# RG-LRU gates as four 64x64 quadrants of the TensorE array in place of 128x128 block-diagonal products

## The chip, the cores and the metric

One NeuronCore of a Trainium2 chip runs the whole program as one launch. The metric is the device time of an execution in microseconds (us); a comparison uses the median of several executions. Engines are named as in the profile: PE is TensorE (PEld its weight loads), DVE is VectorE, ACT is ScalarE, SP is SyncE, which issues the transfers here.

## What is computed

The reference is one inference step of a two-layer decoder trunk, with 1,024 prompt tokens and 8 sample tokens (1,032 columns in all), width 1,024, all in float32. Layer 0 has an SSD mixer and a gMLP mixer, layer 1 a Conformer convolution and an RG-LRU. The change concerns the two gates of the RG-LRU:

```python
xc, buf_new = _causal_dwconv(xd, conv_buf, conv_w, conv_b)
xb = xf.reshape(bsz, L, D_HEADS, D_BLOCK)          # 16 heads of 64 channels
r = sigmoid(einsum('blhi,hij->blhj', xb, wa).reshape(bsz, L, W) + ba)
i = sigmoid(einsum('blhi,hij->blhj', xb, wx).reshape(bsz, L, W) + bx)
log_a = -LRU_C * r * softplus(-lam)
a = exp(log_a)
bterm = sqrt(-expm1(2.0 * log_a)) * (i * xf)
# h[t] = a[t] * h[t-1] + bterm[t], then the gate path and the output projection
```

Each head has its own 64x64 weight matrix for `r` and for `i`.

## The kernel before

Activations lie channel by channel: a tile has 128 channels on its partitions and the 1,032 tokens along it. The tokens are cut into three chunks of 344 columns (`CH`). The large projections are done by `unit` and `chunk` (lines 107 to 123): for each block of 128 output channels, and each chunk, 24 products of 128x128 by 344 columns run into one PSUM bank (`mm_...`, lines 115 to 117). They are three products for each of eight blocks of input channels, since inputs and weights are split into a rounded part and the rest. Four banks belong to these (`mm`), two each to the pools `sA` and `sB`.

Layer 1 alternates over eight blocks of 128 channels (`ORDER`, line 27): `c_block(j)` for the Conformer convolution (projections `gb` and `ga`, then a convolution of 31 taps, L859, that VectorE does at low priority) and `d_block(j)` for the RG-LRU (projections `xd` and `gd`, a convolution of 4 taps, the gates, the scan). A block of 128 channels holds two heads. So lines 809 to 818 build `bd`, a 128x128 block-diagonal matrix for each gate and block, out of a memset and 32 transfers of 64x64, and `d_block` does for each gate `m` and chunk `c` one product of 128x128 and one activation (lines 880 to 885), through a bank of `sA`:

```python
pg = bank("sA", f"gt{j}{m}{c}")
T.matmul(pg[:, :CH], bd[:, m, j % 4, :], xc[:, cs], start=True, stop=True)
S.activation(t[:, cs], pg[:, :CH], AF.Sigmoid, bias=pcol(bn, j))
```

The tile framework orders each engine's instructions by priority and by its own estimate of when they are ready; the order is fixed when the program is built. The products of the gates of block `j` thus stand among those of `c_block(j + 1)`.

Two other places have products that use a part of the array. `ssd_group` in layer 0 (lines 459 to 464) writes head `h` to partitions 0 to 63 or 64 to 127 of the tile `py`, by `h % 2`: a product of 128 rows and 64 columns with `x0` (L462) and, from the second chunk on, one with the state `st` (L464). And `csT` (line 412) has 16 columns:

```python
dst = py[r0:r0 + 64, (h // 2) * P:(h // 2 + 1) * P]
T.matmul(dst, x0[:, h, :], cb_b[:, h, :], start=True, stop=c == 0)
if c:
    T.matmul(dst, st[:, h * 64:(h + 1) * 64], ce[:, h, :], start=False, stop=True)
```

After the eight blocks come the sums over the convolution's channels (`sum_cln`, lines 164 to 173 and 918 to 920), which need the last taps of VectorE, and the two output projections (`od`, `oc`).

Of the kernel before, what the change touches and what calls it, by code (L numbers as in the profile page):

```python
# [10 lines left out]
AF = mybir.ActivationFunctionType  # L11
OP = mybir.AluOpType

P = 128
# [3 lines left out]
CH = NT // 3  # L18
NB = 8
# [25 lines left out]
def tile_trunk(ctx, tc, a, o):  # L45
    nc = tc.nc
    V, S, T, G, SY = nc.vector, nc.scalar, nc.tensor, nc.gpsimd, nc.sync
# [8 lines left out]
    def blk(tag, name, shape=None, dt=F32):  # L56
        return hp.tile(shape or [P, NT], dt, name=name, tag=tag, bufs=NTAG[tag])

    def bank(tag, name):
        return pp.tile([P, 512], F32, name=name, tag=tag, bufs=4 if tag == "mm" else 2)  # L60
# [59 lines left out]
    def unit(src, xs, name, evac, k0=0):  # L120
        w = load_w(src, name)
        for c in range(3):
            chunk(w, xs, c, name, evac, k0)
# [5 lines left out]
    def act_evac(dst, func, **kw):  # L129
        def f(ps, cs):  # L130
            S.activation(dst[:, cs], ps, func, **kw)  # L131
        return f

    def copy_evac(dst):
        def f(ps, cs):
            S.copy(dst[:, cs], ps)
        return f
# [43 lines left out]
    xts, ws = [], []  # L181
# [58 lines left out]
    def pcol(name, j, k=0):  # L240
        return pc[:, j, PROW[name] + k:PROW[name] + k + 1]
# [38 lines left out]
    def tail_rows(t, lo, n, name, *outs):  # L280
        ps = bank("sA", "tl_" + name)
        T.transpose(ps[:n, :P], t[:, lo:lo + n], ident)
        rows = rowt("rows_" + name)
        S.copy(rows[:n], ps[:n, :P])
        i = 0
        for dst in outs:
            m = dst.shape[0]
            SY.dma_start(dst, rows[i:i + m])
            i += m

    def conv4(rw, dst, w, bcol, srow, j):
        pw, pb = PROW[w], PROW[bcol]
        col = lambda k: pc[:, j, pw + k:pw + k + 1]
        S.activation(dst, rw, AF.Identity, bias=pc[:, j, pb:pb + 1], scale=col(3))
        for k in range(3):
            d = 3 - k
            V.scalar_tensor_tensor(dst[:, d:L], rw[:, :L - d], col(k), dst[:, d:L], op0=OP.mult, op1=OP.add)
        st = sc[:, j, srow:srow + 24].rearrange("p (b k) -> p k b", k=3)
        for k in range(3):
            V.scalar_tensor_tensor(dst[:, L:], st[:, k, :], col(k), dst[:, L:], op0=OP.mult, op1=OP.add)  # L300
# [382 lines left out]
    def z_unit(j):  # L683
        t = blk("mt", f"sz{j}")
        unit(w_in_e[:, ZC + j * P:ZC + (j + 1) * P], hn, f"z{j}", act_evac(t, AF.Silu))
        V.tensor_mul(xy[j], xy[j], t)
        S.activation(t, xy[j], AF.Square)
        return t
# [13 lines left out]
    for g in range(2):  # L702
        acc = None
        for i in range(4):
            t = z_unit(g * 4 + i)
# [8 lines left out]
        for i in range(4):  # L714
            j = g * 4 + i
# [90 lines left out]
    V.tensor_scalar(cvec[:, :, 0], spl, -8.0, None, op0=OP.mult)  # L806
    V.tensor_scalar(cvec[:, :, 1], spl, 8.0, None, op0=OP.mult)

    bds = []
    for q, tag in enumerate(("S", "ws")):  # L810
        bd = blk(tag, f"bd{q}", [P, 2, 4, P])
        V.memset(bd, 0.0)
        for m, wn in enumerate(("lru_wa", "lru_wx")):
            for e in range(2):
                src = a[wn]
                for i in range(4):
                    SY.dma_start(bd[e * 64:(e + 1) * 64, m, i, e * 64:(e + 1) * 64], src[0, 2 * (q * 4 + i) + e])
        bds.append(bd)

    def c_block(j):  # L820
        sb = blk("xy", f"gl{j}")
# [47 lines left out]
    def d_block(j):  # L869
        js = slice(j * P, (j + 1) * P)  # L870
        rw = blk("mt", f"rwd{j}")
        unit(w_in_o[:, XDC + j * P:XDC + (j + 1) * P], hn, f"xd{j}", copy_evac(rw))
        tail_rows(rw, L - 3, 11, f"lc{j}", o["lru_conv_prompt"][0, 0, :, js], o["lru_conv_sample"][0, :, 2, js])
        xc = blk("mt", f"xc{j}")
        conv4(rw, xc, "lru_conv_w", "lru_conv_b", S_LRUC, j)
        sgd = blk("ld", f"sgd{j}")
        unit(w_in_o[:, GDC + j * P:GDC + (j + 1) * P], hn, f"gd{j}", act_evac(sgd, AF.Silu))
        gi = blk("xx", f"gi{j}")
        bd = bds[j // 4]
        for m, (t, bn) in enumerate(((rw, "lru_ba"), (gi, "lru_bx"))):  # L880
            for c in range(3):
                cs = slice(c * CH, (c + 1) * CH)
                pg = bank("sA", f"gt{j}{m}{c}")
                T.matmul(pg[:, :CH], bd[:, m, j % 4, :], xc[:, cs], start=True, stop=True)
                S.activation(t[:, cs], pg[:, :CH], AF.Sigmoid, bias=pcol(bn, j))
        r = rw
        V.tensor_mul(gi, gi, xc)
        av = xc
        S.activation(av, r, AF.Exp, scale=cvec[:, j, 0:1])
        S.activation(r, r, AF.Tanh, scale=cvec[:, j, 1:2])  # L890
        hv = blk("mt", f"hv{j}")
        S.activation(hv, av, AF.Square)
        V.scalar_tensor_tensor(r, hv, 1.0, r, op0=OP.add, op1=OP.mult)
        S.activation(r, r, AF.Sqrt)
        V.tensor_mul(gi, gi, r)
        V.tensor_tensor_scan(hv[:, :L], av[:, :L], gi[:, :L], 0.0, op0=OP.mult, op1=OP.add)
        V.tensor_mul(hv[:, L:], av[:, L:], sc[:, j, S_LRU:S_LRU + NS])
        V.tensor_add(hv[:, L:], hv[:, L:], gi[:, L:])
        tail_rows(hv, L - 1, 9, f"lh{j}", o["lru_prompt"][0, :, js], o["lru_sample"][0, :, js])
        V.tensor_mul(hv, hv, sgd)  # L900
        SY.dma_start(mdd[j], hv)

    cj, dj = iter(range(NB)), iter(range(NB))
    for ch in ORDER:
        c_block(next(cj)) if ch == "c" else d_block(next(dj))
    sgc, md, mc = [], [None] * 8, [None] * 8
    for j in range(NB):
        t = blk("xy" if j < 7 else "S", f"sgc{j}")
        unit(w_in_o[:, GCC + j * P:GCC + (j + 1) * P], hn, f"gc{j}", act_evac(t, AF.Silu))
        sgc.append(t)  # L910
        if j >= 4:
            i = j - 4
# [9 lines left out]
    for i, j in enumerate((4, 5, 6, 7, 0, 1, 2, 3)):  # L922
        t = blk(("xy", "ce")[i % 2], f"cq{j}")
# [13 lines left out]
    for j in (4, 5, 6, 7, 0, 1, 2, 3):  # L937
        if j < 4:
            t = blk("bc", f"cr{j}")
            SY.dma_start(t, ccd[j])  # L940
            V.tensor_sub(t, t, mean)
        else:
            t = cs_t[j]
# [102 lines left out]
```

## Time and profile before

| what | us |
|---|---|
| device time, median of 3 executions (lowest to highest) | 1519.19 (1517.06 to 1519.57) |
| profiled execution: span from first to last instruction (the profile gives no other time of it) | 1515.8 |
| TensorE busy | 1497.5 |
| VectorE busy | 1058.3 |
| ScalarE busy | 702.7 |

The span leaves out what lies before the first and after the last instruction, so it stands a little below the device times. Busy shares are averages over stages of different kinds; the stage of the change is the stretch from 870 to 1270 us, in which the eight `d_block`s have their gates. In a timeline the length of a TensorE record includes the way through the array, so records overlap, and the distance between starts is what one of them takes from the queue.

### The profile page before, as it was taken

How to read it: one execution, taken by the hardware profiler on the slowest of the kernel's cores; microseconds unless marked ns; L12 is line 12 of the kernel's file. 1: busy time of each engine (PE TensorE's matmuls, PEld its weight loads, DVE VectorE, ACT ScalarE, POOL GpSimd, SP SyncE). 2: the span in 40 equal slices, each digit the busy share in tenths (PEclk: the TensorE clock that was granted, in tenths of full speed). 3: DMA queues.
4: the chain of work that ended last, by engine and by line, in shares of the span. 5: the costliest groups of instructions: out<-in, count | busy, mean ns of one | idle time of the engine just before them, and what ended most of it. 6: DMA issues, size and time to landing. Idle time of an engine off the chain costs nothing.

```text
span 1515.8 us, 23657 instructions
## 1 busy us (share of the span) xinstructions
PE 1497.5 (99%) x9844; PEld 1464.1 (97%) x9844; DVE 1058.3 (70%) x1486; ACT 702.7 (46%) x1049; POOL 0.9 (0%) x7
## 2 busy tenths in 40 slices
PE   7999999999999999999999999999999999999998
PEld 6899999999999999999999999999999999999997
DVE  6535666568767862542437799999999999867524
ACT  6557666585654333420224445354445447334213
POOL 0000000000000000000000000000000000000000
PEclk9999999999999999999999999999999999999999
DMA  6225322233325661244432212221121221457402
GB/s 199 70 75 141 117 76 85 68 125 113 112 98 173 210 198 53 70 160 148 157 96 91 57 46 84 74 75 60 57 75 45 66 62 54 156 183 235 156 28 113
DMA packets 180193, 161.52 MB, mean 107 GB/s; under 512 B 11624, under 2 KB 159772, under 8 KB 180054
## 3 DMA queue, kind: packets, MB, share of 16 engines
q1 hardware_dynamic: 180086, 160.01, 33.5%
q8 instruction: 77, 1.26, 0.3%
q14 instruction: 30, 0.25, 0.1%
HBM read 118.91 MB, written 42.18 MB: 106 GB/s over the span
## 4 chain that ended last, share of the span: by engine, by line
PE 97%; ACT 1%; DVE 1%; DMA 0%; issue 0%; SPq 0%; DVEq 0%
PE mm_x L115 2%; PE mm_xd L115 2%; PE mm_x L117 2%; PE mm_xd L117 2%; PE mm_ob L116 2%; PE mm_od L115 2%; PE mm_z L115 2%; PE mm_oa L115 2%; PE mm_z L117 2%; PE mm_x L116 2%; PE mm_od L116 2%; PE mm_gd L115 2%; PE mm_u L115 2%; PE mm_ob L115 2%; PE mm_g L115 2%; PE mm_oc L115 2%
## 5 line engine op out<-in xcount | busy, mean ns | idle before, releaser
L859 DVE SCALAR_TENSOR_TENSOR c<-gl,pc,c 128x1017 f32<-128x1017 f32 (+25 forms) x240 | 294.7, 1262 | 0.9
L116 PE MATMUL mm_gb<-hnl,wh_gb 128*128 128x344 f32 x192 | 63.5, 331 | 0.3 <-DVE hnl L127 0.3
L115 PE MATMUL mm_gb<-hnh,wh_gb 128*128 128x344 f32 x192 | 63.1, 329 | 0.3 <-ACT gl L131 0.3
L115 PE MATMUL mm_xd<-hnh,wh_xd 128*128 128x344 f32 x192 | 62.6, 326 | 0.7 <-ACT wh_xd L103 0.7
L115 PE MATMUL mm_ga<-hnh,wh_ga 128*128 128x344 f32 x192 | 63.3, 329 | 0.0
L115 PE MATMUL mm_u<-hnh,wh_u 128*128 128x344 f32 x192 | 62.6, 326 | 0.0
L117 PE MATMUL mm_gb<-hnh,wl_gb 128*128 128x344 f32 x192 | 62.4, 325 | 0.0
L115 PE MATMUL mm_v<-hnh,wh_v 128*128 128x344 f32 x192 | 62.4, 325 | 0.0
L117 PE MATMUL mm_ga<-hnh,wl_ga 128*128 128x344 f32 x192 | 62.4, 325 | 0.0
L117 PE MATMUL mm_v<-hnh,wl_v 128*128 128x344 f32 x192 | 62.2, 324 | 0.0
L116 PE MATMUL mm_v<-hnl,wh_v 128*128 128x344 f32 x192 | 62.1, 324 | 0.0
L116 PE MATMUL mm_ga<-hnl,wh_ga 128*128 128x344 f32 x192 | 62.1, 324 | 0.0
L116 PE MATMUL mm_gc<-hnl,wh_gc 128*128 128x344 f32 x192 | 62.0, 323 | 0.0
L117 PE MATMUL mm_x<-hnh,wl_x 128*128 128x344 f32 x192 | 62.0, 323 | 0.0
L115 PE MATMUL mm_gc<-hnh,wh_gc 128*128 128x344 f32 x192 | 61.9, 323 | 0.0
L117 PE MATMUL mm_xd<-hnh,wl_xd 128*128 128x344 f32 x192 | 61.9, 324 | 0.0
L115 PE MATMUL mm_x<-hnh,wh_x 128*128 128x344 f32 x192 | 61.9, 322 | 0.0
L117 PE MATMUL mm_gd<-hnh,wl_gd 128*128 128x344 f32 x192 | 61.8, 322 | 0.0
L116 PE MATMUL mm_x<-hnl,wh_x 128*128 128x344 f32 x192 | 61.8, 322 | 0.0
L116 PE MATMUL mm_u<-hnl,wh_u 128*128 128x344 f32 x192 | 61.7, 321 | 0.0
L115 PE MATMUL mm_g<-hnh,wh_g 128*128 128x344 f32 x192 | 61.7, 321 | 0.0
L116 PE MATMUL mm_g<-hnl,wh_g 128*128 128x344 f32 x192 | 61.7, 321 | 0.0
(476 smaller groups left out, 4932.5 us busy)
## 6 DMA issues: line engine op xcount, KB each, us to landing
x<-res SPq DMA_DIRECT2D x16, 516.0 KB
csb<-csd SPq DMA_DIRECT2D x16, 512.0 KB
mbd<-u SPq DMA_DIRECT2D x8, 516.0 KB
mbl<-mbd SPq DMA_DIRECT2D x8, 516.0 KB
rb<-res SPq DMA_DIRECT2D x8, 516.0 KB
res<-rb SPq DMA_DIRECT2D x8, 516.0 KB
res<-x SPq DMA_DIRECT2D x8, 516.0 KB
mdd<-hv SPq DMA_DIRECT2D x8, 516.0 KB
```

The lines of the kernel that those rows point to most:

```text
L115: T.matmul(out, wh[:, k, :], xh[:, cs], start=i == 0, stop=False)
L116: T.matmul(out, wh[:, k, :], xl[:, cs], start=False, stop=False)
L117: T.matmul(out, wl[:, k, :], xh[:, cs], start=False, stop=i == NB - 1)
L859: V.scalar_tensor_tensor(c[:, d:L], gl[:, :L - d], w(k), c[:, d:L], op0=OP.mult, op1=OP.add)
```

## The change

The zero blocks go. One tile `gwt` holds the 64x64 matrices, those of even heads on partitions 0 to 63 and of odd heads on 64 to 127, and four transfers fill it; the memsets go too. A new helper `gates` does the work of a block. For each chunk it takes both banks of `sA`, `pg[0]` for the even head `e = 0` and `pg[1]` for the odd one, and runs four products of 64x64 by 344 columns. Gate `m` of head `e` reads rows `64 e` and writes columns `64 (e ^ m)`, so that the four use the four quadrants of the array. Four activations of 64 partitions follow, in place of two of 128; they put the result back on the partitions of its head. The arithmetic is the same.

```diff
--- before.py
+++ after.py
@@ -806,16 +806,26 @@
     V.tensor_scalar(cvec[:, :, 0], spl, -8.0, None, op0=OP.mult)
     V.tensor_scalar(cvec[:, :, 1], spl, 8.0, None, op0=OP.mult)
 
-    bds = []
-    for q, tag in enumerate(("S", "ws")):
-        bd = blk(tag, f"bd{q}", [P, 2, 4, P])
-        V.memset(bd, 0.0)
-        for m, wn in enumerate(("lru_wa", "lru_wx")):
-            for e in range(2):
-                src = a[wn]
-                for i in range(4):
-                    SY.dma_start(bd[e * 64:(e + 1) * 64, m, i, e * 64:(e + 1) * 64], src[0, 2 * (q * 4 + i) + e])
-        bds.append(bd)
+
+    gwt = blk("S", "gwt", [P, 2, NB, 64])
+    for m, wn in enumerate(("lru_wa", "lru_wx")):
+        src = a[wn][0].rearrange("(j e) i o -> e i j o", e=2)
+        for e in range(2):
+            SY.dma_start(gwt[e * 64:(e + 1) * 64, m], src[e])
+
+    def gates(j, xc, r, gi):
+
+
+        for c in range(3):
+            cs = slice(c * CH, (c + 1) * CH)
+            pg = [bank("sA", f"gt{j}{c}{e}") for e in range(2)]
+            rows = [slice(e * 64, (e + 1) * 64) for e in range(2)]
+            for m in range(2):
+                for e in range(2):
+                    T.matmul(pg[e][rows[e ^ m], :CH], gwt[rows[e], m, j, :], xc[rows[e], cs], start=True, stop=True)
+            for m, (t, bn) in enumerate(((r, "lru_ba"), (gi, "lru_bx"))):
+                for e in range(2):
+                    S.activation(t[rows[e], cs], pg[e][rows[e ^ m], :CH], AF.Sigmoid, bias=pcol(bn, j)[rows[e]])
 
     def c_block(j):
         sb = blk("xy", f"gl{j}")
@@ -876,13 +886,7 @@
         sgd = blk("ld", f"sgd{j}")
         unit(w_in_o[:, GDC + j * P:GDC + (j + 1) * P], hn, f"gd{j}", act_evac(sgd, AF.Silu))
         gi = blk("xx", f"gi{j}")
-        bd = bds[j // 4]
-        for m, (t, bn) in enumerate(((rw, "lru_ba"), (gi, "lru_bx"))):
-            for c in range(3):
-                cs = slice(c * CH, (c + 1) * CH)
-                pg = bank("sA", f"gt{j}{m}{c}")
-                T.matmul(pg[:, :CH], bd[:, m, j % 4, :], xc[:, cs], start=True, stop=True)
-                S.activation(t[:, cs], pg[:, :CH], AF.Sigmoid, bias=pcol(bn, j))
+        gates(j, xc, rw, gi)
         r = rw
         V.tensor_mul(gi, gi, xc)
         av = xc
```

The change moves instructions of several engines. In the names below `gt` is followed by block, gate and chunk before, and by block, chunk and half `e` after.

TensorE, chunk 0 of block 0, among the products of `gb1`; before:

```order
L116 MATMUL mm_gb1_0_8399<-hnl_89,wh_gb1_8389 128x344
L884 MATMUL gt000_8349<-xc0_8255,bd0_7908 128x344
L884 MATMUL gt001_8352<-xc0_8255,bd0_7908 128x344
L117 MATMUL mm_gb1_0_8399<-hnh_88,wl_gb1_8390 128x344
L115 MATMUL mm_gb1_0_8399<-hnh_88,wh_gb1_8389 128x344
```

And now:

```order
L115 MATMUL mm_gb1_0_8380<-hnh_88,wh_gb1_8370 128x344
L825 MATMUL gt000_8318<-xc0_8224,gwt_7908 64x344
L825 MATMUL gt001_8319<-xc0_8224,gwt_7908 64x344
L825 MATMUL gt000_8318<-xc0_8224,gwt_7908 64x344
L825 MATMUL gt001_8319<-xc0_8224,gwt_7908 64x344
L116 MATMUL mm_gb1_0_8380<-hnl_89,wh_gb1_8370 128x344
```

Two 128x128 products, one gate each for one chunk and the next, have become four quadrants of one chunk that stand together.

TensorE, the same block, around its next chunk; before:

```order
L115 MATMUL mm_gb1_1_8425<-hnh_88,wh_gb1_8389 128x344
L884 MATMUL gt002_8355<-xc0_8255,bd0_7908 128x344
L116 MATMUL mm_gb1_1_8425<-hnl_89,wh_gb1_8389 128x344
L117 MATMUL mm_gb1_1_8425<-hnh_88,wl_gb1_8390 128x344
L884 MATMUL gt010_8358<-xc0_8255,bd0_7908 128x344
L115 MATMUL mm_gb1_1_8425<-hnh_88,wh_gb1_8389 128x344
```

And now:

```order
L117 MATMUL mm_gb1_1_8406<-hnh_88,wl_gb1_8371 128x344
L825 MATMUL gt010_8328<-xc0_8224,gwt_7908 64x344 x2
L115 MATMUL mm_gb1_1_8406<-hnh_88,wh_gb1_8370 128x344
L116 MATMUL mm_gb1_1_8406<-hnl_89,wh_gb1_8370 128x344
L825 MATMUL gt011_8329<-xc0_8224,gwt_7908 64x344 x2
L117 MATMUL mm_gb1_1_8406<-hnh_88,wl_gb1_8371 128x344
```

Where single products stood, two quadrants of one half `e` stand together, then two full products, then the two of the other half. All eight blocks have this pattern: one group of four, then four groups of two, with two to 22 full products between groups of a block.

VectorE, at the last taps of the convolution (`c7`), with the splits of reloaded tiles (`hnl`) and the last sum `cacc`; before:

```order
L104 TENSOR_TENSOR wl_od1_12404<-wr_od1_12401,wh_od1_12403 128x1024
L859 SCALAR_TENSOR_TENSOR c7_11204<-gl7_11029,pc_319,c7_11204 128x996
L127 TENSOR_TENSOR hnl_89<-mdl6_12181,hnh_88 128x1032
L859 SCALAR_TENSOR_TENSOR c7_11204<-gl7_11029,pc_319,c7_11204 128x995
L127 TENSOR_TENSOR hnl_89<-mdl7_12185,hnh_88 128x1032
L859 SCALAR_TENSOR_TENSOR c7_11204<-gl7_11029,pc_319,c7_11204 128x994
L865 TENSOR_TENSOR cacc_8161<-cacc_8161,c7_11204 128x1032
L732 TENSOR_TENSOR rd0_12320<-mm_od0_0_12322,rd0_12320 128x344
L732 TENSOR_TENSOR rd0_12320<-mm_od0_1_12348,rd0_12320 128x344
L127 TENSOR_TENSOR sl_cln_12190<-cacc_8161,sh_cln_12189 128x1032
```

And now:

```order
L104 TENSOR_TENSOR wl_od0_12382<-wr_od0_12379,wh_od0_12381 128x1024
L869 SCALAR_TENSOR_TENSOR c7_11257<-gl7_11082,pc_319,c7_11257 128x997
L869 SCALAR_TENSOR_TENSOR c7_11257<-gl7_11082,pc_319,c7_11257 128x996
L869 SCALAR_TENSOR_TENSOR c7_11257<-gl7_11082,pc_319,c7_11257 128x995
L869 SCALAR_TENSOR_TENSOR c7_11257<-gl7_11082,pc_319,c7_11257 128x994
L875 TENSOR_TENSOR cacc_8130<-cacc_8130,c7_11257 128x1032
L127 TENSOR_TENSOR hnl_89<-mdl4_12238,hnh_88 128x1032
L127 TENSOR_TENSOR hnl_89<-mdl5_12242,hnh_88 128x1032
L127 TENSOR_TENSOR sl_cln_12255<-cacc_8130,sh_cln_12254 128x1032
```

The four `hnl` splits, of which two are in the piece of before, stand behind `cacc` now. On TensorE the first product of `sum_cln` has 2,899 products of layer 1's projections ahead of it, in place of 2,976.

## Rows read from the trace of the kernel before

**Rows 1.** The page: busy time of each engine, and the chain that ended last by engine.

```profile
PE 1497.5 (99%) x9844; PEld 1464.1 (97%) x9844; DVE 1058.3 (70%) x1486; ACT 702.7 (46%) x1049; POOL 0.9 (0%) x7
...
PE 97%; ACT 1%; DVE 1%; DMA 0%; issue 0%; SPq 0%; DVEq 0%
```

**Rows 2.** 870 to 1270 us: length, busy PE, PEld, DVE, ACT, POOL; clock; DMA.

```profile
870.00:1270.00 400.00, 400.00 (x2473) 389.21 (x2472) 382.48 (x380) 194.07 (x262) 0.00 (x0) 1.00 0.21 62
```

**Rows 3.** What TensorE waited for, 60 to 1460 us, longest first (total, times, longest).

```profile
PE mm_xd L115 <- ACT wh_xd L103: 0.7, 1, 0.7
```

**Rows 4.** The tile `gt`: its instructions (count: nanoseconds min/median/max, first and last start, shape).

```profile
L884 PE MATMUL gt<-xc,bd x96: 450/452/459, 876.1 to 1256.7; 128*128 128x344 f32 x96
L885 ACT ACTIVATE rwd<-gt,pc x24: 541/548/552, 876.8 to 1252.7; 128x344 f32<-128x344 f32 x24
```

**Rows 5.** The chain of waits around the first gate products (start, length, what).

```profile
876.23 1.16 PE gt L884 x4
```

**Rows 6.** Timeline of TensorE at 173 us, `py` (start, length, instruction, shapes, records).

```profile
173.38 0.45 PE L462 MATMUL py<-csb,x 128*64 128x128 f32 x4
173.65 0.40 PE L464 MATMUL py<-ce,st 128*64 128x128 f32 x4
173.87 0.44 PE L462 MATMUL py<-csb,x 128*64 128x128 f32 x4
...
174.96 0.44 PE L464 MATMUL py<-ce,st 128*64 128x128 f32 x4
```

**Rows 7.** Timeline of TensorE at 311 us, from `mm_v` over `py` to `pn`.

```profile
311.19 0.32 PE L115 MATMUL mm_v<-hnh,wh_v 128*128 128x344 f32 x1
311.44 1.09 PE L462 MATMUL py<-csb,x 128*64 128x128 f32 x16
...
312.80 0.40 PE L471 MATMUL pn<-x,bth 128*128 128x512 f32 x1
313.04 0.39 PE L472 MATMUL pn<-x,btl 128*128 128x512 f32 x1
313.27 0.32 PE L116 MATMUL mm_v<-hnl,wh_v 128*128 128x344 f32 x1
```

**Rows 8.** Timeline of TensorE at 80 us, from `mm_x` over `csT` and back.

```profile
80.21 0.32 PE L116 MATMUL mm_x<-hnl,wh_x 128*128 128x344 f32 x1
80.46 1.05 PE L412 MATMUL csT<-tri,dA 128*16 128x128 f32 x8
...
81.70 0.32 PE L115 MATMUL mm_x<-hnh,wh_x 128*128 128x344 f32 x1
81.86 0.32 PE L116 MATMUL mm_x<-hnl,wh_x 128*128 128x344 f32 x1
```

**Rows 9.** Lines 412 (`csT`) and 462 (`py`): their weight loads.

```profile
L412 PEld LDWEIGHTS csT<-tri,dA x16: 92/97/97, 75.5 to 81.1; 128*16 128x16 f32 x16
L462 PEld LDWEIGHTS py<-csb,x x256: 132/137/137, 157.8 to 450.3; 128*64 128x64 f32 x128
```

**Rows 10.** Line 284, shapes apart: ScalarE's copies of few partitions.

```profile
L284 ACT COPY rows_cc<-tl_cc x8: 250/251/259, 855.5 to 1231.8; 38x128 f32<-38x128 f32 x8
...
L284 ACT COPY rows_lh<-tl_lh x8: 238/255/258, 905.1 to 1284.7; 9x128 f32<-9x128 f32 x8
```

**Rows 11.** Timeline of ScalarE at the first gate activations (in brackets: idle before, releaser).

```profile
876.85 1.12 ACT L885 ACTIVATE rwd<-gt,pc 128x344 f32<-128x344 f32 x2 [0.24 <-PE gt L884]
```

**Rows 12.** Lines 817 and 812: transfers and memsets that build the gate weights.

```profile
L817 SPq DMA_DIRECT2D bd<-in_lru_wx_dram x16: 477/595/605, 832.8 to 847.9; - x16
L812 DVE MEMSET bd<- x2: 912/912/912, 826.2 to 827.3; 128x1024 f32 x2
```

**Rows 13.** Timelines around the sums of the convolution: VectorE, ScalarE, TensorE.

```profile
1323.22 1.23 DVE L865 TENSOR_TENSOR cacc<-cacc,c 128x1032 f32<-128x1032 f32 x1
1324.49 1.06 ACT L126 CAST sh_cln<-cacc 128x1032 fp32r<-128x1032 f32 x1 [4.59 <-DVE cacc L865]
1328.69 0.47 PE L170 MATMUL sum_cln<-sh_cln,one1r 128*128 128x344 f32 x2
```

## The prediction

> **What bounds the kernel now.** I first read the page's engine line and its chain of waits [rows 1]: TensorE is busy 99% of the span, and 97% of the chain that ends last is TensorE's own work. Then the stretch in which the gate products run, 870 to 1270 us, by engine [rows 2]: TensorE is busy for 400.00 of its 400 us at the full granted clock (1.00, the 2.4 GHz level), VectorE for 382 and ScalarE for 194. The list of what TensorE waited for, from 60 us to 1460 us, has four entries, of which the longest is 0.7 us [rows 3]. So the kernel is one queue of matrix products, and a microsecond that TensorE gains or loses between 870 and 1270 us appears in the end, unless it then runs into somebody who is late.
>
> **What goes.** There are 48 gate products (8 blocks, 3 chunks, 2 gates). Each float32 product is two records in the trace: the 48 are 96 records [rows 4]. On the chain, four records take 1.16 us [rows 5], so a product takes 0.58 us and the 48 take 48 x 0.58 = 27.8 us, none of it hidden.
>
> **What comes: streaming.** There are 96 products of a 64x64 block with the same 344 columns, so each again takes 0.58 us by itself; a gain comes only from products that run side by side in different parts of the array. The trace has such products: `py` (L462 and L464) writes heads to partitions 0 to 63 and 64 to 127 in turn. The program puts L462 and L464 of one head (same half) behind each other, and then those of the next head. In the trace the first row is four records of L462, that is two heads at once, before any L464 [rows 6]; eight such rows follow each other. From 173.87 to 174.96 us there are 5 rows of 4 records, or 20 records in 1.09 us, 0.109 us for each pair. A record of 128 columns alone should take 0.29 x 128/344 = 0.108 us. So the two halves run fully side by side, and TensorE looks far enough ahead to fill both.
>
> The order decides how many run together. I count five groups in each block: one with all four quadrants (chunk 0), then four with two quadrants (the halves of chunks 1 and 2), with two to 22 other products between them. That is 8 groups of four and 32 of two, 40 in all. If every group takes the time of one product, streaming takes 40 x 0.58 = 23.2 us, 4.6 us less than now. Only the eight groups of four gain; a pair of quadrants does half a chunk in the time in which one full product did one gate of it.
>
> **What comes: changing the array's division.** Each group is a small island between full 128x128 products. Two places of the trace show such islands. At 311 us [rows 7] the time from the last product before `py` (311.19) to the second `pn` (312.80) is 1.61 us. In it lie one product's pitch (0.16, from 81.70 to 81.86 in [rows 8]), eight pairs (8 x 0.109 = 0.872) and one `pn` (0.235, half of 312.80 to 313.27): 0.34 us are left over. At 80 us [rows 8] `csT` takes 81.70 - 80.21 = 1.49 us, less two pitches (0.32) and eight records one after the other (0.872): 0.30 us are left over. Entering and leaving therefore costs 0.30 to 0.34 us. `csT` loads weights of 16 columns and `py` of 64, and the loads take 97 and 137 ns [rows 9]; the longer one fits the dearer island. A quadrant has 64 weight columns, so I take 0.34: 40 x 0.34 = 13.6 us. The 128x128 gate products pay nothing of this now: their 1.16 us for four records is pure streaming at 0.29.
>
> No row shows an island that is divided in rows and columns at once. The lower end for its price is `csT`'s 0.30. For the upper end I allow as much above `py` as `csT` lies below it, 0.38.
>
> **The sum.** -27.8 + 23.2 + 13.6 = **+9.0 us** (+7.4 at 0.30 and +10.6 at 0.38). On the profiled execution's span of 1515.8 us that is 1524.8. The median of the runs, 1519.2 us, is 3.4 above this span; I add the same there and predict **1528.2 us**.
>
> **What I cost at nothing, and its cover.** ScalarE gets 96 activations of 64 partitions for 48 of 128. Partitions don't make them shorter: a copy of 9x128 takes as long as one of 38x128 [rows 10]. At 0.548 us [rows 4] that is 26 us more on ScalarE, which has 206 us free in this stretch [rows 2]. Do its later releases hold TensorE? Half-chunk 0 of chunk 1 needs the bank that chunk 0's first two activations empty. ScalarE now starts 0.75 us after the product (876.1 to 876.85) [rows 4, 11], so the bank is free at 0.75 + 2 x 0.55 = 1.85 us. TensorE comes back for it after its own group (0.58 + 0.34) and 23 products at 0.16, 4.6 us. The cover is 2.7 us; without it each late bank would stop the whole queue.
>
> The 32 weight transfers become four. They occupied SyncE for about 0.59 us each from 827 us on, and the two memsets took 0.91 us of VectorE each [rows 12]; nothing waits for either, and the first gate product is 28 us after the last of them was issued (847.9). I cost both at nothing.
>
> The third place of the order could turn into a new wait. The sums of the convolution (`sum_cln`) stand 77 products earlier in TensorE's queue (2,899 products of the odd layer's projections ahead of them, 2,976 before), so TensorE reaches them at 1328.7 - 77 x 0.16 + 9.0 = 1325.4 us. Their input `sh_cln` was ready at 1325.55 [rows 13]. VectorE now has four splits (1.23 us, as the `cacc` row of the same shape) and two memsets less to do before it, 6.7 us: ready at about 1318.8, so nothing waits. What is late next is nobody.
>
> **The rivals.**
> 1. *The change of division costs nothing for quadrants, and the kernel gets faster.* Then only streaming counts: -4.6 us, 1514.6 us. It turns at 4.6/40 = 0.115 us for a group. Against it: both islands cost three times that [rows 7, 8]; for it, only that neither is a quadrant. TensorE would then also meet `sum_cln` 7 us before VectorE is through, which would eat part of the gain. The Trainium skill goes further: "TensorEngine Tiling (Array Packing)", section Theoretical Speedup, has each dimension of 64 double the rate. By it the 96 products would take a quarter of 55.7 us, 13.9, and the time would be 1505.3 us. The trace agrees for two halves of columns, but the order has only eight groups of four.
> 2. *Half of it is hidden* (0.17 us for each group): +2.3 us, 1521.5 us, hardly to be told from no change. For it: between the two pairs of a chunk lie only two to four full products.
> 3. *The two halves of rows don't run together* (both write the same partitions, in two banks). Each group of four takes two steps: 8 x 0.58 = 4.6 us more, +13.6, 1532.8 us. No row shows two products in different rows of the array at once, so nothing excludes it.
> 4. *The quadrants don't run side by side as intended.* If each record started only when the one before it in the program had started on its part, two records of one quadrant would hold up the next quadrant: a pair takes three records (0.87), a four five (1.45): 32 x 0.87 + 8 x 1.45 = 39.4 us of streaming, +25.2, 1544.4 us. If all ran alone: 96 x 0.58 = 55.7, +41.5, 1560.7 us. Against both: `py` overtakes its own program order [rows 6]. The Trainium skill, "TensorE: Matmul & The Clock Gate", Part 3, The mechanism, says that products start and end strictly in program order. By that rule the first of these two holds and the time would be 1544.4 us; this trace disagrees, since L462 of the second head starts before L464 of the first, and the measurement decides.
>
> **How the numbers follow.** Forecast (+7.4 to +10.6): 0.64, since both prices that go into it were read in this very program. Rival 3: 0.12. Rival 2: 0.09. Rival 1: 0.08. Rival 4: 0.07. The range from 1523.5 to 1534.0 holds the forecast, rival 3 and the upper part of rival 2, together 0.80. A measurement of this kernel can tell about 0.2% (3 us) from no change. Faster is rival 1 less what VectorE may eat, 0.07; the same is most of rival 2 and that rest, 0.09; slower is all else, 0.84.
>
> **What would show it.** Right: `gt` in 40 islands, each about 0.92 us from the product before to the product after, less their pitch; in the groups of four, four records starting within a few hundredths of a microsecond; TensorE still without waits. Rival 3: in a group of four, two records at a time. Rival 1: the product behind an island starts at its usual pitch. The forecast is wrong if the islands cost under 0.2 us each, or if a wait at `gt` or `sum_cln` appears in TensorE's list.

## The result, and the profile after

| | before | changed |
|---|---|---|
| median of 5 runs, us | 1517.42 | 1527.18 |
| lowest to highest, us | 1515.96 to 1519.57 | 1526.47 to 1527.60 |
| span of the profiled execution, us | 1515.8 | 1525.5 |

The changed kernel is slower: the ratio is 1.0062 [1.0051, 1.0074], +9.8 us. Predicted were +9.0 us and 1528.2 us from the earlier median of 1519.2.

The page of the changed kernel (busy time of each engine, chain of waits by engine), the stretch from 870 to 1270 us, and what TensorE waited for from 60 to 1460 us:

```profile
PE 1506.2 (99%) x9940; PEld 1452.5 (95%) x9940; DVE 1057.0 (69%) x1484; ACT 732.3 (48%) x1099; POOL 0.9 (0%) x7
...
PE 97%; ACT 1%; DVE 1%; DMA 0%; issue 0%; SPq 0%; DVEq 0%
```

```profile
870.00:1270.00 400.00, 398.55 (x2499) 367.06 (x2498) 378.70 (x376) 213.76 (x300) 0.00 (x0) 1.00 0.20 62
```

```profile
PE mm_gd L115 <- ACT rwd L136: 0.9, 1, 0.9
PE xT L228 <- ACT xo L229: 0.7, 1, 0.7
PE mm_gd L115 <- ACT sgd L131: 0.5, 1, 0.5
PE mm_xd L115 <- ACT wh_xd L103: 0.5, 1, 0.5
```

Beside [rows 1, 2, 3]: the chain is still 97% TensorE, its clock still 1.00, and TensorE is busy for 8.7 us more. ScalarE has 29.6 us more, VectorE 1.3 us less. New are the two waits of `mm_gd`, 1.4 us; they are the 1.45 us that TensorE lacks in the stretch, where it had none before.

The tile `gt` (count, nanoseconds min/median/max, first and last start, shape), which answers to [rows 4]:

```profile
L825 PEld LDWEIGHTS gt<-xc,gwt x192: 129/131/133, 874.8 to 1266.3; 64*64 64x64 f32 x192
L828 ACT ACTIVATE rwd<-gt,pc x48: 530/544/548, 877.1 to 1269.5; 64x344 f32<-64x344 f32 x48
```

The 192 records are 96 products of a quadrant, in place of 48 products; a weight load of 64 columns takes 131 ns, near `py`'s 137 [rows 9]; half the partitions leave an activation at 544 ns, where the full one took 548.

The timeline of TensorE at the first group of four quadrants, and at a group of two (start, length, instruction, records):

```profile
874.59 0.31 PE L115 MATMUL mm_gb<-hnh,wh_gb 128*128 128x344 f32 x1
874.83 0.81 PE L825 MATMUL gt<-xc,gwt 64*64 64x344 f32 x8
875.57 0.42 PE L116 MATMUL mm_gb<-hnl,wh_gb 128*128 128x344 f32 x1
875.83 0.32 PE L117 MATMUL mm_gb<-hnh,wl_gb 128*128 128x344 f32 x1
```

```profile
880.37 0.32 PE L116 MATMUL mm_gb<-hnl,wh_gb 128*128 128x344 f32 x1
880.62 0.80 PE L825 MATMUL gt<-xc,gwt 64*64 64x344 f32 x4
881.35 0.42 PE L117 MATMUL mm_gb<-hnh,wl_gb 128*128 128x344 f32 x1
881.61 0.32 PE L115 MATMUL mm_gb<-hnh,wh_gb 128*128 128x344 f32 x1
```

Eight records (four quadrants) take 0.81 us and four records (two quadrants) 0.80: all quadrants of a group run at once. An island is such a group between full products, and a pitch is the 0.16 us from start to start of full products. From the start of the product before an island to the start of the second product after it are 875.83 - 874.59 = 1.24 us, and at the group of two 881.61 - 880.37 = 1.24 as well; the other islands lie within 0.02 us of this. Less two pitches (0.32) that is 0.92 us: the 0.58 of one product and 0.34 for entering and leaving. 40 islands take 36.8 us where the 48 products had taken 27.8: +9.0 us.

Of quadrants running at once the Trainium skill says, in "TensorE: Matmul & The Clock Gate", Part 3, The mechanism, that a pack spans one product and a few nanoseconds for each further tile: the 0.81 us beside 0.80 agree. For the price of an island, "TensorEngine Tiling (Array Packing)", Key Properties, says that a change of mode, and not of tile alone, drains TensorE; it gives no duration. This trace agrees that the change of mode is what costs, 0.34 us for an island, while `py` goes from half to half without loss [rows 6]; whether TensorE is drained at it no run here shows.

### The profile page after: what moved, and what is told of

The parts are those of the page before. It is cut to its first block, busy times and chain, and to the rows that moved or that the text cites. A ratio compares the mean times of both kernels' runs of the same rounds, so it can differ in the third digit from the quotient of the medians.

```text
span 1525.5 us, 23862 instructions
## 1 busy us (share of the span) xinstructions
PE 1506.2 (99%) x9940; PEld 1452.5 (95%) x9940; DVE 1057.0 (69%) x1484; ACT 732.3 (48%) x1099; POOL 0.9 (0%) x7
## 3 DMA queue, kind: packets, MB, share of 16 engines
q8 instruction: 78, 1.28, 0.4%
## 4 chain that ended last, share of the span: by engine, by line
PE 97%; ACT 1%; DVE 1%; DMA 0%; issue 0%; SPq 0%; DVEq 0%
PE mm_ga L115 2%; PE mm_gb L116 2%; PE mm_ga L117 2%; PE mm_xd L115 2%; PE mm_xd L117 2%; PE mm_gb L117 2%; PE mm_gb L115 2%; PE mm_x L115 2%; PE mm_gc L115 2%; PE mm_x L117 2%; PE mm_oa L115 2%; PE mm_ga L116 2%; PE mm_gc L116 2%; PE mm_od L117 2%; PE mm_gc L117 2%; PE mm_ob L116 2%
## 5 line engine op out<-in xcount | busy, mean ns | idle before, releaser
L869 DVE SCALAR_TENSOR_TENSOR c<-gl,pc,c 128x1017 f32<-128x1017 f32 (+21 forms) x240 | 294.9, 1263 | 1.1
L115 PE MATMUL mm_gd<-hnh,wh_gd 128*128 128x344 f32 x192 | 61.9, 322 | 1.4 <-ACT rwd L136 0.9
```

The source lines that it names most:

```text
L115: T.matmul(out, wh[:, k, :], xh[:, cs], start=i == 0, stop=False)
L869: V.scalar_tensor_tensor(c[:, d:L], gl[:, :L - d], w(k), c[:, d:L], op0=OP.mult, op1=OP.add)
```

## The experiments

The kernel before was run again each time: 1517.29 us (median of 21 runs) beside experiments 1 to 4 and 1517.33 us (of 8) beside 5 and 6. Differences are against these. Experiments 1 to 5 came out within the range of the theory that was written down before, 6 did not.

**1. ScalarE's part alone.** On the kernel before, each activation is split into two of 64 partitions; the products stay.

```diff
-                S.activation(t[:, cs], pg[:, :CH], AF.Sigmoid, bias=pcol(bn, j))
+                for e in range(2):
+                    es = slice(e * 64, (e + 1) * 64)
+                    S.activation(t[es, cs], pg[es, :CH], AF.Sigmoid, bias=pcol(bn, j)[es])
```

> The kernel before, its 48 full 128x128 gate products untouched, but each gate activation split in two of 64 partitions, as in the change (96 activations of 64x344 in place of 48 of 128x344). My theory: the loss of the change (+9.8 us) lies in entering and leaving the divided array, and ScalarE's doubled work is covered; so no change, -1.5 to +1.5 us against the kernel before (1517.4), and gt still 0.29 us for each record. Rival theory: the later release of the sA banks by ScalarE holds TensorE up; then most of the +9.8 us appears here, without any divided product, and as waits of TensorE in front of gt.

Measured: 1518.46 us, ratio 1.0008 [1.0000, 1.0017], +1.2 us (0.0 to 2.6). What TensorE waited for, the longest row:

```profile
PE mm_gd L115 <- ACT sgd L131: 1.1, 2, 0.5
```

A wait of `mm_gd` is there too, without a divided product, so it comes with the split activations. They can account for about 1 us of the loss, and hardly for more than 2.6; the rest must lie elsewhere, and the rows above place it in TensorE's islands.

**2. Divided in rows alone: one 64x128 product for each head.** On the changed kernel, both gates' weights of a head stand side by side, so a chunk has two products in the two halves of rows, and islands have half as many products.

```diff
-    gwt = blk("S", "gwt", [P, 2, NB, 64])
+    gwt = blk("S", "gwt", [P, NB, 2, 64])
...
-            for m in range(2):
-                for e in range(2):
-                    T.matmul(pg[e][rows[e ^ m], :CH], gwt[rows[e], m, j, :], xc[rows[e], cs], start=True, stop=True)
+            for e in range(2):
+                T.matmul(pg[e][:, :CH], gwt[rows[e], j].rearrange("p m o -> p (m o)"), xc[rows[e], cs], start=True, stop=True)
```

(The transfers that fill `gwt` and the rows that the activations read are changed to match; these lines are left out.)

> The change, but each head's two gates are one product of 64 rows by 128 columns (48 products, tile 64x128), so the array is divided by rows only; again 40 islands, 8 of two products and 32 of one. Streaming stays 40 x 0.58 = 23.2 us. If the first weight load of an island is what is exposed, and it grows with the weight columns (0.05 us for 64, 0.11 for 128), an island costs 0.40 instead of 0.34 us: 2 us more than the change, +11 to +13 us against the kernel before. If the price is a fixed one of dividing the array: as the change, +9 to +10.5 us. If a division by rows costs nothing: -5 to -3 us.

Measured: 1529.01 us, ratio 1.0076 [1.0064, 1.0089], +11.7 us. Weight loads, and the timeline of TensorE at an island of one product:

```profile
L824 PEld LDWEIGHTS gt<-xc,gwt x96: 182/184/187, 874.6 to 1273.6; 64*128 64x128 f32 x96
```

```profile
878.95 0.31 PE L117 MATMUL mm_gb<-hnh,wl_gb 128*128 128x344 f32 x1
879.19 0.84 PE L824 MATMUL gt<-xc,gwt 64*128 64x344 f32 x2
879.97 0.43 PE L115 MATMUL mm_gb<-hnh,wh_gb 128*128 128x344 f32 x1
880.23 0.32 PE L116 MATMUL mm_gb<-hnl,wh_gb 128*128 128x344 f32 x1
```

1.28 us less 0.32 and 0.58 leaves 0.38 us for this island; the median of the 40 is 0.39. So the price grows with the columns of the weights: 0.30 us at 16 columns (load 97 ns), 0.34 at 64 (131 ns), 0.39 at 128 (184 ns). The loads differ by 87 ns from first to last and the islands by 90. The sum is 40 x (0.58 + 0.39) - 27.8 = +11.0 us, and with TensorE's waits, 2.7 us in all against 2.0 [rows 3], +11.7. The measured time alone (+9.7 to +13.5 us by its interval) would not exclude the upper end of a fixed price; the rows of the islands do.

The rows also show where the price grows. `csT`'s island needs one more row of before, beside [rows 8]:

```profile
81.44 0.43 PE L117 MATMUL mm_x<-hnh,wl_x 128*128 128x344 f32 x1
```

From the product before an island to its first product are 0.24 to 0.25 us in all three kinds, 0.08 to 0.09 more than a pitch, and from the first full product after it to the second 0.26, 0.10 more. What differs lies between these: 0.98 - 0.87 = 0.11 us for `csT`, 0.73 - 0.58 = 0.15 for quadrants, 0.78 - 0.58 = 0.20 here, each within 0.02 us of one weight load. The loads of the changed kernel at the island of 880.62 us:

```profile
880.62 0.20 PEld L825 LDWEIGHTS gt<-xc,gwt 64*64 64x64 f32 x4 [0.22 <-issue]
881.35 0.19 PEld L117 LDWEIGHTS mm_gb<-hnh,wl_gb 128*128 128x128 f32 x1 [0.53 <-issue]
881.45 0.19 PEld L115 LDWEIGHTS mm_gb<-hnh,wh_gb 128*128 128x128 f32 x1
```

The first load of the island and the first behind it start together with their products (880.62 and 881.35), while the next starts 0.16 us ahead of its own (881.45 for 881.61). So the first load of an island is not hidden behind products; why it starts no earlier, no run shows.

**3. Fewer islands: three banks from two pools.** On the changed kernel, chunk 1 takes its banks from another pool, so that it no longer waits for chunk 0's to come free.

```diff
-            pg = [bank("sA", f"gt{j}{c}{e}") for e in range(2)]
+            pg = [bank(("sA", "sB", "sA")[c], f"gt{j}{c}{e}") for e in range(2)]
```

> The change, with the banks of chunk 1 taken from the pool sB, so that chunks 0 and 1 are free at once: in each block one island of eight quadrants and two of two, 24 islands in place of 40 and 32 steps of 0.58 us in place of 40; 96 products and 96 activations as in the change. My theory (price for each island, 0.34 us, and 0.58 us for each step): 24 x 0.34 + 32 x 0.58 = 26.7 us against 27.8 of the kernel before: -1 us, between -2.5 and +0.5; 9 to 11 us faster than the change. Rival theory (each of the 96 small products costs more than its share, wherever it stands): as slow as the change, +8 to +11 us.

Measured: 1516.77 us, ratio 0.9996 [0.9987, 1.0005], -0.5 us. The timeline of TensorE at the first island of eight quadrants:

```profile
873.47 0.32 PE L116 MATMUL mm_gb<-hnl,wh_gb 128*128 128x344 f32 x1
873.72 1.39 PE L825 MATMUL gt<-xc,gwt 64*64 64x344 f32 x16
875.04 0.43 PE L117 MATMUL mm_gb<-hnh,wl_gb 128*128 128x344 f32 x1
875.31 0.32 PE L115 MATMUL mm_gb<-hnh,wh_gb 128*128 128x344 f32 x1
```

Eight products in 1.84 - 0.32 = 1.52 us: two times 0.58, and 0.36 for the island. The second step of four quadrants adds 1.39 - 0.81 = 0.58 us. The order has 8 islands of eight and 16 of two: 8 x 1.52 + 16 x 0.92 = 26.9 us, 0.9 less than the 27.8 and 9.9 less than the change's 36.8. Of these 9.9 us about 5.4 are the 16 islands that are gone (at 0.34), and 4.6 the 8 steps that two pairs now share (at 0.58). The 96 products and 96 activations are the same, so the loss is not a price of each small product, as the rival has it.

**4. Fewer still: chunks of 8, 512 and 512 columns.** The same two pools, and wider chunks.

```diff
-        for c in range(3):
-            cs = slice(c * CH, (c + 1) * CH)
-            pg = [bank("sA", f"gt{j}{c}{e}") for e in range(2)]
+        for c, (lo, n) in enumerate(((1024, 8), (0, 512), (512, 512))):
+            cs = slice(lo, lo + n)
+            pg = [bank(("sA", "sB", "sA")[c], f"gt{j}{c}{e}") for e in range(2)]
```

(`:n` stands for `:CH` in the products and activations.)

> As the run with islands of eight, but the gates are cut into 512 + 512 + 8 columns, the eight sample columns first (pools sA, sB, sA): 16 islands, one of eight products (four of 8 and four of 512 columns) and one of four of 512 in each block. My theory: 16 x 0.34 + 16 x 0.86 (512 columns) + 8 x about 0.15 (8 columns) = 20.4 us against 27.8: -7.4 us, between -9 and -5, about 1510: faster than both kernels. Rival theory (price for each product): 96 products as in the change, no faster than the kernel before.

Measured: 1509.65 us, ratio 0.9949 [0.9936, 0.9963], -7.6 us: faster than both kernels. Its two kinds of island on TensorE's timeline:

```profile
874.12 0.32 PE L116 MATMUL mm_gb<-hnl,wh_gb 128*128 128x344 f32 x1
874.37 1.21 PE L825 MATMUL gt<-xc,gwt 64*64 64x512 f32 x16
875.51 0.43 PE L117 MATMUL mm_gb<-hnh,wl_gb 128*128 128x344 f32 x1
875.78 0.32 PE L115 MATMUL mm_gb<-hnh,wh_gb 128*128 128x344 f32 x1
...
878.14 0.32 PE L115 MATMUL mm_gb<-hnh,wh_gb 128*128 128x344 f32 x1
878.39 1.09 PE L825 MATMUL gt<-xc,gwt 64*64 64x512 f32 x8
879.41 0.42 PE L116 MATMUL mm_gb<-hnl,wh_gb 128*128 128x344 f32 x1
879.67 0.32 PE L117 MATMUL mm_gb<-hnh,wl_gb 128*128 128x344 f32 x1
```

Less two pitches, the first takes 1.66 - 0.32 = 1.34 us (the narrow chunk and a wide one, 16 records) and the second 1.53 - 0.32 = 1.21. Every quadrant of a chunk now stands beside the other three. 8 x (1.34 + 1.21) = 20.4 us, 7.4 less than before. Of the gain of half the streaming (27.8 / 2 = 13.9 us), 16 islands take 16 x 0.35 = 5.6, and the narrow chunk's products the rest.

**5. Islands without a gain.** On the kernel before, each block-diagonal product becomes two of 64 columns with the same 128 rows, zeros included. Two run side by side in the time of one; nothing is saved.

```diff
-                T.matmul(pg[:, :CH], bd[:, m, j % 4, :], xc[:, cs], start=True, stop=True)
+                for e in range(2):
+                    es = slice(e * 64, (e + 1) * 64)
+                    T.matmul(pg[es, :CH], bd[:, m, j % 4, es], xc[:, cs], start=True, stop=True)
```

> The kernel before, with each 128x128 gate product done as two products of 128 rows by 64 columns (the block-diagonal matrix with its zeros stays, 96 products), so that the array is divided with nothing to gain in streaming: 48 steps of 0.58 us as before, in 40 islands. My theory: 40 x 0.34 = +13.6 us against the kernel before, +12 to +15. Rival theory (a product of 64 columns costs more by itself, 0.39 us for each of the 96 as the change's total of 37.6 us would have it): +9 to +11 us.

Measured: 1531.37 us, ratio 1.0093 [1.0078, 1.0108], +14.0 us. The timeline of TensorE over two islands:

```profile
879.91 0.32 PE L117 MATMUL mm_gb<-hnh,wl_gb 128*128 128x344 f32 x1
880.16 0.80 PE L886 MATMUL gt<-xc,bd 128*64 128x344 f32 x4
880.89 0.43 PE L115 MATMUL mm_gb<-hnh,wh_gb 128*128 128x344 f32 x1
881.25 0.80 PE L886 MATMUL gt<-xc,bd 128*64 128x344 f32 x4
881.97 0.43 PE L116 MATMUL mm_gb<-hnl,wh_gb 128*128 128x344 f32 x1
882.24 0.32 PE L117 MATMUL mm_gb<-hnh,wl_gb 128*128 128x344 f32 x1
```

From 879.91 to 882.24 are 2.33 us, less three pitches (0.48) 1.85 for two islands, 0.925 each: 0.58 + 0.345. Here too are 40 islands, and 40 x 0.345 = 13.8. The price belongs to the island, whether it is divided in columns alone or into quadrants.

**6. The gate products left out.** On the changed kernel the products are left out, and the activations read `xc` in their place.

```diff
-            pg = [bank("sA", f"gt{j}{c}{e}") for e in range(2)]
...
-            for m in range(2):
-                for e in range(2):
-                    T.matmul(pg[e][rows[e ^ m], :CH], gwt[rows[e], m, j, :], xc[rows[e], cs], start=True, stop=True)
...
-                    S.activation(t[rows[e], cs], pg[e][rows[e ^ m], :CH], AF.Sigmoid, bias=pcol(bn, j)[rows[e]])
+                    S.activation(t[rows[e], cs], xc[rows[e], cs], AF.Sigmoid, bias=pcol(bn, j)[rows[e]])
```

> The change without its gate products: the activations read the convolved input xc in place of them, so the gates r and i are not the reference's; everything else stays. If TensorE alone set the time, all of its 36.6 us in islands would go: -27.8 us against the kernel before, about 1490. If VectorE (382 of 400 us busy in this stretch) or ScalarE takes over as soon as TensorE is that much earlier, part of it turns into waits of TensorE in front of later products: my theory is a gain of only 10 to 22 us, with waits of several us in TensorE's list, none of them at gt.

Measured: 1510.53 us, ratio 0.9958 [0.9944, 0.9972], -6.8 us, outside the expected gain. All 27.8 us of the 48 products are gone from TensorE's queue, and most come back as waits of TensorE (the two longest rows). Behind them stands a wait of ScalarE (the row below them, from 1225 to 1310 us):

```profile
PE mm_gc L115 <- ACT sgc L131: 17.0, 3, 15.9
PE tl_lh L282 <- DVE hv L898: 3.1, 2, 1.6
```

```profile
ACT sgc L131 <- DVE c L865: 11.3, 2, 10.1
```

`mm_gc` needs a bank that the activation `sgc` empties, and `sgc` waits for VectorE's convolution `c`. The long wait also costs clock. The stretch from 1271 to 1287 us (length; busy PE, PEld, DVE, ACT, POOL; granted clock; DMA), and two products of TensorE's timeline:

```profile
1271.00:1287.00 16.00, 2.92 (x10) 2.92 (x11) 16.00 (x15) 2.21 (x4) 0.00 (x0) 0.50 0.27 83
```

```profile
1284.08 0.65 PE L115 MATMUL mm_gc<-hnh,wh_gc 128*128 128x344 f32 x1 [15.95 <-ACT sgc L131]
...
1287.39 0.32 PE L117 MATMUL mm_gc<-hnh,wl_gc 128*128 128x344 f32 x1
```

VectorE is busy for all 16 us. TensorE stood still for 15.95 us, the granted clock fell to 0.50 (the 1.2 GHz level), and the 11 products from 1284.08 to 1287.39 took 3.3 us where 11 pitches are 1.7, which is about 1.6 us lost. TensorE's waits are 21.5 us in all against 2.0: 27.8 - 19.5 - 1.6 = 6.7 us of gain are left, beside 6.8 measured. So in this order, which brings TensorE there so early, VectorE is the bound. It is not the most that the gate products can be worth: experiment 4, which has all of them, is 0.9 us faster than this run, in another order. Whether experiment 4 stands near such a bound was not measured: its waits of TensorE are no longer than before.

## Why the prediction was right

- **What goes, 27.8 us:** the rows of before told it, and the account of experiment 6, which starts from it, closes to 0.1 us.
- **Streaming, 23.2 us:** held. Four quadrants take the time of two (0.81 and 0.80 us), and a further step takes 0.58 us (experiment 3). Rivals 3 and 4 fall: neither do the halves of rows take turns, nor do second records hold up the next quadrant.
- **40 islands at 0.34 us, 13.6 us:** held, with the value taken from `py` and not the end from `csT`. Halves of 128x64 cost the same as quadrants (experiment 5), and the price follows the weight columns (experiment 2). Experiments 3 and 4 show it from the other side, with fewer steps as well as fewer islands: with 24 islands the loss is gone, with 16 it is a gain. Rivals 1 and 2 fall with each island's rows.
- **ScalarE at nothing:** nearly. The cover for `gt`'s banks held: no wait at `gt`. The cost was elsewhere, and the sign "TensorE still without waits" did not quite come true. ScalarE in the changed kernel, at 1215 us:

```profile
1214.81 0.54 ACT L828 ACTIVATE gi<-gt,pc 64x344 f32<-64x344 f32 x1
1215.37 1.28 ACT L131 ACT_TABLE_LOAD   x1
1217.72 0.46 ACT L131 ACTIVATE sgd<-mm_gd 128x344 f32<-128x344 f32 x1 [1.07 <-PE mm_gd L117]
1218.20 1.28 ACT L893 ACT_TABLE_LOAD   x1
...
1222.71 1.12 ACT L136 COPY rwd<-mm_xd 128x344 f32<-128x344 f32 x3
```

`mm_gd` starts at 1218.23, when `sgd` has emptied its bank, and again at 1223.18, when the first of the three copies of `mm_xd` has, which stood behind two table loads and the long activations: 0.55 + 0.90 us. The same tile waits for 1.1 us in experiments 1 and 2, which also have split activations, and not in 5, which has not. But 3 and 4 have them too and no such wait: it takes the split activations and an order in which they meet `mm_gd`. In all, TensorE's waits are 2.6 us against 2.0 before, so 0.6 us are added: 9.0 + 0.6 = 9.6, and the spans differ by 9.7.
- **`sum_cln` at nothing:** held, with less room than was worked out. Rows of the tiles `sum_cln` and `sh_cln`, and one row each of VectorE's and ScalarE's timelines, which answer to [rows 13]:

```profile
L170 PEld LDWEIGHTS sum_cln<-sh_cln,one1r x3: 187/188/189, 1325.6 to 1331.8; 128*128 128x128 f32 x3
...
L126 ACT CAST sh_cln<-cacc x1: 1052/1052/1052, 1321.6 to 1321.6; 128x1032 fp32r<-128x1032 f32 x1
```

```profile
1318.92 1.23 DVE L875 TENSOR_TENSOR cacc<-cacc,c 128x1032 f32<-128x1032 f32 x1
```

```profile
1319.68 2.01 ACT L126 CAST hnh<-mdl 128x1032 fp32r<-128x1032 f32 x2
```

TensorE reached it at 1325.6, as foreseen (1325.4). But `sh_cln` was ready at 1322.6 and not at 1318.8, for two reasons. VectorE began the last `cacc` 4.3 us earlier than before (1318.92 against 1323.22) and not 6.7, which is about what the four splits take without the memsets. And when `cacc` was done, at 1320.15, ScalarE was at two casts of `hnh`, so the cast `sh_cln` began 1.4 us later. The room was 3 us and not 6.6.

The predicted time lies 1.0 us above the measured median, though the difference was 0.8 us too small: the median of before was 1519.19 in the three runs shown then, and 1517.42 over five. That the two errors have opposite signs is luck. Three slips in the working change nothing in its sum: rival 2 adds up to +2.2 us and not +2.3, up to 23 and not 22 products stand between groups of a block, and one of the eight blocks has 12 full products between the two pairs of a chunk, not two to four.

## What to carry to other kernels

Count the times that TensorE's array changes its division, not only the columns that are streamed: here each island costs 0.30 to 0.39 us, more than half of a product of 344 columns. Here packing paid only where the order and the free banks left the packed products next to each other, so look to the banks first: the same quadrants went from +9.8 to -7.6 us with banks from two pools and wider chunks. Where one engine is busy for 99%, look up who is second before you hope for more.

## What the runs showed of the hardware that was not expected

- The price of an island follows the weight columns: 0.30 us at 16 (in the trace of before), 0.34 at 64, 0.39 at 128, beside weight loads of 97, 131 and 184 ns. The first load stands uncovered, and the part that is the same in all three is about 0.2 us; no run varied that part at a fixed load.
- Two products in different halves of rows that write the same partitions in two banks run at once, without any loss (0.81 us for four quadrants).
- Taking 27.8 us of products from an engine that is busy for 99% gained only 6.8 us: 19.5 us came back as waits, and a single wait of 16 us brought the granted clock from 1.00 to 0.50, which cost about 1.6 us more.
